# A hybrid decoder step on one core: sample gates loaded early by SyncE, middle tokens' norms ahead of the sample group's, output tiles stored in halves

## The chip, the core and the metric

The kernel runs on one core of a Trainium2 chip. The core has five engines with queues of their own: TensorE (PE in the profile; PEld is its weight load), VectorE (DVE), ScalarE (ACT), GpSimd (POOL) and SyncE (SP), and 16 DMA engines that they share. The metric is the device time of one execution in microseconds, from the chip's own clock; the kernel is timed over several runs, and one execution more is recorded by the hardware profiler.

## What is computed

One layer of a decoder with two kinds of attention heads side by side, for a prompt of 1024 new tokens and a sample group of 8 x 8 new tokens that have 4096 past tokens each. All data are float32. Cut to what matters here:

```python
def project(x, norm_g, w_in, q_g, ks_g, kw_g):
    h = rms_norm(x, norm_g)                 # over D_MODEL = 1024
    z = h @ w_in                            # 3864 columns
    (q_a, k_a, v_a, gate_a, q_b, kc, vc, ks, vs, kw, vw, br, gate_b) = jnp.split(z, split_at, axis=-1)
    ...
    br = jax.nn.sigmoid(br.reshape(B, T, NSA_HEADS, 3))

def decoder_layer(...):
    o_sb = stick_breaking(q_a, ...)         # over past and new rows
    o_nsa = nsa_attend(q_b, br, ...)        # gates br weigh compressed, selected and window attention
    u = concat([o_sb * silu(gate_a), o_nsa * silu(gate_b)])
    h = x + u @ w_out
    y = h + sigmoid(h @ w_ple_gate) * (p @ w_ple)
```

## The kernel before

The 1768.8 us fall into five stretches. Up to some 550 us `phase1` normalizes the tokens and multiplies them with `w_in`, from some 390 us on mixed with stick-breaking units of the prompt (`phase_d`). From 550 to 590 the prompt's rows are compressed (`prompt` in `phase_c`). From 590 to 985 `phase_c` goes through the eight sample sequences (batches of some 47 us): it gathers 1 MB pieces of the paged cache, compresses them and scores them. From 985 to 1510 come the stick-breaking attention of the sample group (`phase_b`) and the prompt's second kind of heads (the rest of `phase_d`), mixed. From 1510 on the output projections run (`a` and `b` of the last class).

**phase1.** The 1024 prompt tokens are nine tiles `x` with the sample group: tile 0 to 7 of 128 tokens, tile 8 of 64. `xnorm(ts)` (L135 on) normalizes one or two tiles: a square sum of the even one on ScalarE (L143), of the odd one on VectorE (L141), the small statistics on VectorE and ScalarE (L67 to L72), and the scaling on VectorE (L149) and GpSimd (L147). `xtrans(t0, n)` (L151 on) transposes two tiles on TensorE in eight k steps (L155); each step is then split into a high part `hh` (ScalarE, L157) and a low part `hl` (VectorE, L158). The matmuls of L278 multiply these with the weights, which `wsplit` splits into `whi` (GpSimd, L122) and `wlo` (VectorE, L123). In the text the order is: pair 0/1, pair 2/3, sample tile 8 with its transposes (L178) and split (L180 to L182), pair 4/5, pair 6/7.

**Gates of the sample group.** `phase1` writes the raw gates `br` to the scratch tensor `s_br_s`. At its start after the prompt's compression, `phase_c` makes two small tiles: `cgtc` (64 x 24) is filled by eight loads of 64 runs of 12 bytes each (L617, issued by ScalarE), `sigmoid_small` takes Exp on ScalarE (L57), add and reciprocal on VectorE (L58, L59), and four copies make `cgts` (L620). They are read in every batch. Around them stand ScalarE's table load for Tanh (L516), the casts XH (L491), GpSimd's or VectorE's XL (L496) and the matmuls H (L510).

**Output.** In `b` (L1709) two halves n of 512 columns are computed one after the other into one tile `y` (one buffer), and ScalarE issues one store of 512 KB a tile (L1726), 256 KB for the sample tile.

**What sets the order.** A scheduler that simulates the engines orders each engine's instructions, in the order in which they can start by its model. In `phase_c` from its start to the middle of batch 6 the order is written out by hand instead. SyncE and ScalarE issue the plain DMAs, GpSimd the gathers; the DMAs of SyncE and ScalarE share eight semaphores in turn, and a DMA waits until the earlier one on its semaphore has landed.

Of the kernel before, what the change touches and what calls it, by code (L numbers as in the profile page):

```python
# [5 lines left out]
F32 = mybir.dt.float32  # L6
# [14 lines left out]
def hbm(ap, off, dims):  # L21
    return bass.AP(tensor=ap.tensor, offset=ap.offset + off, ap=[list(d) for d in dims])
# [61 lines left out]
def phase1(K, beside=None):  # L84

    nc, A = K.nc, K.A
    with ExitStack() as es:
# [63 lines left out]
        def xtrans(t0, n):  # L151
            for k in range(8):
                pt = ps.tile([128, 512], F32, name="pt", bufs=2)[:, 0:n * 128]
                for i in range(n):
                    nc.tensor.transpose(pt[:, i * 128:(i + 1) * 128], xt[t0 + i][:, k * 128:(k + 1) * 128], K.id)  # L155
                o = slice(t0 * 128, (t0 + n) * 128)
                K.last_hh = nc.scalar.activation(hh[:, k, o], pt, AF.Copy, scale=gT[:, k:k + 1])  # L157
                nc.vector.scalar_tensor_tensor(hl[:, k, o], pt, gT[:, k:k + 1], hh[:, k, o].bitcast(F32), op0=OP.mult, op1=OP.subtract)  # L158
# [12 lines left out]
        for k in range(2, 8, 2):  # L171
            wsplit(0, k)
        xnorm([2, 3])
        xtrans(2, 2)
        xnorm([8])
        pt = ps.tile([128, 512], F32, name="pt", bufs=2)
        for k in range(8):
# [2 lines left out]
        nc.vector.tensor_tensor(tmp, pt.rearrange("p (k t) -> p k t", k=8), gT.unsqueeze(2).to_broadcast([128, 8, 64]), op=OP.mult)  # L180
        nc.scalar.copy(hs[:, :, 0:64], tmp)
        nc.vector.tensor_tensor(hs[:, :, 64:128], tmp, hs[:, :, 0:64].bitcast(F32), op=OP.subtract)  # L182
        for t in (4, 6):
            xnorm([t, t + 1])
            xtrans(t, 2)
        nc.vector.tensor_scalar(gq, gq, 0.125, None, op0=OP.mult)
        xes.close()

# [108 lines left out]
def c_consts(K, cst):  # L297


    nc, A = K.nc, K.A  # L300
# [4 lines left out]
    C.Qb = [cst.tile([128, 2, 2, 4, 4, 8], F32, name=f"cQb{i}") for i in range(2)]  # L305
    for t in C.Qb:
        V.memset(t, 0.0)
    C.W2 = cst.tile([128, 2, 2, 64], F32, name="cw2")
    for kv, n in enumerate("kv"):
        nc.scalar.dma_start(C.W2[:, kv], hbm(A["cmp_w2_" + n], 0, [[64, 128], [128 * 64, 2], [1, 64]]))  # L310
# [139 lines left out]
def phase_c(K, es, esr, tail, more):  # L450
# [160 lines left out]
    for t in kz + [VN]:  # L611
        G.memset(t, 0.0)

    gts = wk.tile([128, 8, 3], F32, name="cgts")
    gtc = wk.tile([64, 8, 3], F32, name="cgtc")
    for h in range(8):
        nc.scalar.dma_start(gtc[h * 8:h * 8 + 8], hbm(T["br_s"], h * 3, [[24, 8], [192, 8], [1, 3]]))  # L617
    sigmoid_small(K, gtc.rearrange("p a b -> p (a b)"))
    for p in range(4):
        V.tensor_copy(gts[p * 32:p * 32 + 32], gtc[(p // 2) * 32:(p // 2) * 32 + 32])  # L620
# [960 lines left out]
class Phase3:  # L1581
# [127 lines left out]
    def b(s, t):  # L1709
        K, A = s.K, s.K.A  # L1710
# [10 lines left out]
        for n in range(2):  # L1721
# [1 line left out]
            S_.activation(y[:m, c], s.product(HX, s.WG, n, 8, S)[:m], AF.Tanh, scale=0.5)  # L1723
            V.scalar_tensor_tensor(y[:m, c], y[:m, c], 1.0, s.product(PX, s.WP, n, 2, S)[:m], op0=OP.add, op1=OP.mult)
            V.scalar_tensor_tensor(y[:m, c], y[:m, c], 0.5, h[:m, c], op0=OP.mult, op1=OP.add)
        nc.scalar.dma_start(hbm(A["y_sample" if S else "y_prompt"], t * 131072 * (not S), [[1024, m], [1, 1024]]), y[:m])  # L1726


EV = tuple(int(x) for x in "1,1".split(","))
# [199 lines left out]
```

## Time and profile before

| | |
|---|---|
| median of 3 runs | 1770.9 us (1770.6 to 1770.93) |
| profiled execution | 1770.6 us |
| its span, first to last instruction | 1768.8 us |
| TensorE busy | 1593.8 us (90%) |
| VectorE busy | 1194.0 us (68%) |
| ScalarE busy | 882.9 us (50%) |
| GpSimd busy | 637.9 us (36%) |
| mean granted TensorE clock | 0.957 of full |

A row of a timeline gives start, duration, engine, line, operation, output and input, and in brackets the idle time before it with what ended it. `x4` joins four instructions of a kind; the duration then runs from the first start to the last end. Matmuls overlap, so their durations are longer than their distance from start to start. "PEclk" is the clock that was granted in a stretch, as a share of 2.4 GHz; 0.50 is 1.2 GHz. ACTq and SPq rows are DMA issues of ScalarE and SyncE.

### The profile page before, as it was taken

To read this page: it belongs to the slowest core of one execution; us is meant where nothing else is said; L and a number is where in the kernel's file an instruction comes from. 1 tells how busy PE (TensorE), PEld (TensorE's weight loads), DVE (VectorE), ACT (ScalarE), POOL (GpSimd) and SP (SyncE) were. 2 spreads that over 40 slices of the span, in tenths; PEclk is the share of its full clock that TensorE was granted. 3 is DMA by queue.
4 is the path that set the end of the run, shared out by engine and by line. 5 is a ranking of instruction groups with operands and counts; after the bars stand their busy time and mean duration, and the time that the engine had idled before them with its cause. 6 is when DMAs were issued, how large, how long until landed. Compare 5 with 4: busy or idle time off the path is not lost.

```text
span 1768.8 us, 41348 instructions
## 1 busy us (share of the span) xinstructions
PE 1593.8 (90%) x15742; PEld 1366.9 (77%) x15742; DVE 1194.0 (68%) x2540; ACT 882.9 (50%) x2220; POOL 637.9 (36%) x1059
## 2 busy tenths in 40 slices
PE   5999999999987799999999688998789887789998
PEld 5999898988876699899988456667567666668887
DVE  7336756877877578788888787676777865573322
ACT  4213645756667334444444478677678777221111
POOL 3123011132313455555553155355345455530000
PEclk9999999999988899999999699899999999799999
DMA  6235132131225465555554997787888874542210
GB/s 199 80 117 161 61 107 92 47 114 59 80 62 119 138 210 189 200 185 199 193 191 136 335 307 275 261 287 269 286 310 295 291 242 138 183 149 77 72 51 36
DMA packets 187080, 300.78 MB, mean 170 GB/s; under 512 B 30265, under 2 KB 100730, under 8 KB 178554
## 3 DMA queue, kind: packets, MB, share of 16 engines
q1 hardware_dynamic: 144930, 206.65, 35.6%
q0 software_dynamic: 9216, 67.11, 11.2%
q10 hardware_dynamic: 32736, 24.38, 4.3%
q8 instruction: 124, 2.03, 0.5%
q14 instruction: 74, 0.61, 0.1%
HBM read 271.81 MB, written 30.48 MB: 171 GB/s over the span
## 4 chain that ended last, share of the span: by engine, by line
PE 37%; DVE 14%; DMA 11%; ACT 6%; issue 5%; POOL 3%; SPq 1%; ACTq 0%; DVEq 0%; POOLq 0%
PE acc L1635 11%; PE H L510 5%; DMA bkv<-in_cache_sb 5%; DMA raw<-in_cache_nsa,cidx 3%; PE pt L1272 2%; PE bz L1394 2%; PE bo L1410 2%; DVE bkT L1488 2%; PE pt L1249 2%; PE sc L682 2%; ACT bAT L1539 1%; PE cav L824 1%; PE acc L278 1%; PE acc L276 1%; DVE xt L486 1%
## 5 line engine op out<-in xcount | busy, mean ns | idle before, releaser
L278 PE MATMUL acc<-whi,hh 128*128 128x256 f32 (+1 forms) x704 | 203.5, 290 | 4.1 <-DVE og L1768 2.5
L278 PE MATMUL acc<-wlo,hh 128*128 128x256 f32 (+1 forms) x704 | 201.0, 287 | 0.0
L278 PE MATMUL acc<-whi,hl 128*128 128x256 f32 (+1 forms) x704 | 199.6, 289 | 0.0
L1488 DVE STREAM_TRANSPOSE bkT<-bkv 128x1024 f32<-128x1024 f32 x128 | 157.5, 1236 | 53.8 <-DMA bkv<-in_cache_sb 37.2
L1240 POOL TENSOR_SCALAR t<-t,nst,gates 128x640 f32<-128x640 f32 (+7 forms) x128 | 107.4, 841 | 107.1 <-DVE nst L1236 71.2
L278 PEld LDWEIGHTS acc<-whi,hh 128*128 128x128 f32 x704 | 134.8, 192 | 6.8 <-POOL whi L122 2.9
L491 ACT CAST XH<-xt 128x512 fp32r<-128x512 f32 x128 | 79.1, 619 | 120.3 <-PE H L510 110.6
L278 PEld LDWEIGHTS acc<-wlo,hh 128*128 128x128 f32 x704 | 134.8, 192 | 0.2 <-issue 0.2
L278 PEld LDWEIGHTS acc<-whi,hl 128*128 128x128 f32 x704 | 132.4, 191 | 0.4 <-issue 0.3
L122 POOL TENSOR_SCALAR whi<-wraw 128x512 fp32r<-128x512 f32 (+1 forms) x60 | 54.0, 925 | 190.3 <-PE acc L248 154.6
L1249 PE MATMUL pt<-idf,t 128*128 128x128 f32 x528 | 95.1, 294 | 17.6 <-ACT u L1766 5.4
L1410 PE MATMUL bo<-bkv,bAT 128*16 128x128 f32 x2048 | 87.7, 289 | 22.5 <-POOL bAT L1541 16.9
L661 POOL DMA_INDIRECT raw<-in_cache_nsa,cidx x64 | 66.0, 1031 | 99.9 <-DVE xt L486 53.3
L1541 POOL TENSOR_SCALAR bAT<-baT 32x128 f32<-32x128 f32 x256 | 76.4, 298 | 71.1 <-DVE baT L1531 37.8
L1766 ACT COPY aT<-pt 128x512 f32<-128x512 f32 (+3 forms) x167 | 77.2, 475 | 35.6 <-PE pt L1050 19.8
L510 PE MATMUL H<-w1hk,XH 128*128 128x256 f32 (+1 forms) x272 | 86.1, 316 | 9.0 <-ACT XH L491 8.2
L1249 PEld LDWEIGHTS pt<-idf,t 128*128 128x128 f32 x528 | 60.5, 146 | 43.7 <-issue 14.2
L1410 PEld LDWEIGHTS bo<-bkv,bAT 128*16 128x16 f32 x2048 | 60.4, 101 | 41.5 <-POOL bAT L1541 27.2
L486 DVE STREAM_TRANSPOSE xt<-raw 128x512 f32<-128x512 f32 x132 | 88.1, 680 | 4.7 <-DMA raw<-out_nsa_rows_prompt 2.9
L1394 PE MATMUL bz<-bkT,bQ 128*32 128x128 f32 x2048 | 84.1, 290 | 7.9 <-DVE bkT L1488 4.5
L1094 DVE TENSOR_TENSOR_SCAN t<-ones,t 128x1024 f32<-128x1024 f32 (+7 forms) x64 | 88.2, 1380 | 0.7
L496 POOL TENSOR_TENSOR XL<-xt,XH 128x512 fp32r<-128x512 f32 x56 | 72.2, 1289 | 38.1 <-ACT XH L491 36.5
(467 smaller groups left out, 5003.1 us busy)
## 6 DMA issues: line engine op xcount, KB each, us to landing
bkv<-in_cache_sb SPq DMA_DIRECT2D x256, 512.0 KB
wraw<-in_w_in SPq DMA_DIRECT2D x28, 512.0 KB
x<-in_x_prompt SPq DMA_DIRECT2D x8, 512.0 KB
out_sb_rows_prompt<-o ACTq DMA_DIRECT2D x32, 128.0 KB
s_gT<-og ACTq DMA_DIRECT2D x16, 256.0 KB
cwin<-in_state_win SPq DMA_DIRECT2D x8, 512.0 KB
wr<-in_w_out SPq DMA_DIRECT2D x16, 256.0 KB
u<-s_uT SPq DMA_DIRECT2D x8, 512.0 KB
```

What stands on the lines that cost most here:

```text
L278: nc.tensor.matmul(acc[:, :w], a[:, k, t * 128:(t + 1) * 128], b[:, k, :w], start=i == 0, stop=i == 23)
L486: V.transpose(xt[:, :, e, :, b], raw[:, :, 0:256].rearrange("p l (k e c) -> p e l k c", e=2, c=32)[:, e])
L491: S_.copy(XH.rearrange("p a b -> p (a b)"), x.rearrange("p e k b s -> p (e k b s)"))
L510: nc.tensor.matmul(H[:m, kv * 256:kv * 256 + 256], x[:, c], y[:, l * 2 + e], start=start and l + kv + e + i == 0, stop=stop and l == 7 and ...
L1094: nc.vector.tensor_tensor_scan(a[:, ::-1], K.ones.to_broadcast([128, W]), a[:, ::-1], 0.0, op0=OP.mult, op1=OP.add)
L1240: (nc.vector if e == "V" else nc.gpsimd).tensor_scalar(x, x, st[:, j:j + 1], gate, op0=OP.mult, op1=OP.mult)
L1249: nc.tensor.transpose(pt[:, b * 128:(b + 1) * 128], x, K.id)
L1394: nc.tensor.matmul(z(h, g), q(j), kT(j), start=jj == 0, stop=jj == 1, skip_group_check=True, tile_position=(0, h * 32))
L1410: nc.tensor.matmul(oav[i * 32:i * 32 + 16], lhs(g, hp), v[:, i * 128:i * 128 + 128], start=first, stop=last, skip_group_check=True, tile_p ...
L1488: V.transpose(t.kT[f][:, :, i % 4:i % 4 + 2].rearrange("p j i t -> p i j t"), kv[:, k:k + 2].rearrange("p i (j c) -> p i j c", j=16))
L1635: nc.tensor.matmul(acc, a, b, start=i == 0, stop=i == len(terms) - 1)
L1766: S_.copy(o, i)
```

## The change

Three edits. In `phase1` the norms of pair 4/5 and 6/7 stand ahead of the sample tile's, the transposes of pair 4/5 directly behind those of pair 2/3, and those of pair 6/7 behind the sample tile's. In `phase_c` the two gate tiles come from the pool of constants and not from the stage's working pool, and the eight loads are issued by SyncE. In `b` the store of a tile becomes two stores of 512 columns, each behind its half, the first by SyncE and the second by ScalarE.

```diff
@@ phase1
         xnorm([2, 3])
+        xnorm([4, 5])
         xtrans(2, 2)
+        xnorm([6, 7])
+        xtrans(4, 2)
         xnorm([8])
...
-        for t in (4, 6):
-            xnorm([t, t + 1])
-            xtrans(t, 2)
+        xtrans(6, 2)
@@ c_consts
+    C.gts = cst.tile([128, 8, 3], F32, name="cgts")
+    C.gtc = cst.tile([64, 8, 3], F32, name="cgtc")
@@ phase_c
-    gts = wk.tile([128, 8, 3], F32, name="cgts")
-    gtc = wk.tile([64, 8, 3], F32, name="cgtc")
+    gts, gtc = C.gts, C.gtc
     for h in range(8):
-        nc.scalar.dma_start(gtc[h * 8:h * 8 + 8], hbm(T["br_s"], h * 3, [[24, 8], [192, 8], [1, 3]]))
+        nc.sync.dma_start(gtc[h * 8:h * 8 + 8], hbm(T["br_s"], h * 3, [[24, 8], [192, 8], [1, 3]]))
@@ b
-        nc.scalar.dma_start(hbm(A["y_sample" if S else "y_prompt"], t * 131072 * (not S), [[1024, m], [1, 1024]]), y[:m])
+            (nc.sync, nc.scalar)[n].dma_start(hbm(A["y_sample" if S else "y_prompt"], t * 131072 * (not S) + n * 512, [[1024, m], [1, 512]]), y[:m, c])
```

The scheduler makes of it an order that differs on all engines at the edited places, and beyond them in two stretches, from some 400 to 590 us and from 985 to 1510 us. The matmuls of `phase_c`'s hand-written part stand as before. Line numbers of the changed kernel are one to three higher.

VectorE in `phase1`, around the second pair's k steps. Before, the splits of the second pair (L158) and of the sample tile (L180, L182) come first, then the norms of the middle pairs (L141 to L149):

```order
L158 SCALAR_TENSOR_TENSOR hl<-pt,gT,hh 128x256 x6
L180 TENSOR_TENSOR junk<-pt,gT 128x512
L141 ISA junk,xss<-x 128x1024
L141 ISA xss 128x1
L182 TENSOR_TENSOR hs<-junk,hs 128x8x64
L67 TENSOR_SCALAR rs<-xss 128x2
L141 ISA junk,xss<-x 128x1024
```

and now the square sums stand between the first pairs' `hl`:

```order
L158 SCALAR_TENSOR_TENSOR hl<-pt,gT,hh 128x256
L67 TENSOR_SCALAR rs<-xss 128x2
L158 SCALAR_TENSOR_TENSOR hl<-pt,gT,hh 128x256
L141 ISA junk,xss<-x 128x1024
L141 ISA xss 128x1
L158 SCALAR_TENSOR_TENSOR hl<-pt,gT,hh 128x256
L70 TENSOR_TENSOR rs<-rs 128x2
```

Two square sums, three groups of statistics and four scalings now lie among the ten `hl` ahead of the third pair's, instead of behind all of the second pair's.

SyncE at 384 us (`nat` are query and key rows of a stick-breaking pair, `vn` its value rows, `wraw` weights of phase1). Before:

```order
L980 DMA nat<-s_qa_p 128x4x128 x2
L980 DMA nat<-out_sb_rows_prompt 128x4x128 x2
L115 DMA wraw<-in_w_in 128x4x256 x4
L1056 DMA vn<-out_sb_rows_prompt 128x8x128
L1111 DMA s_uT<-u 128x1024
```

and now:

```order
L982 DMA nat<-s_qa_p 128x4x128 x2
L982 DMA nat<-out_sb_rows_prompt 128x4x128 x2
L115 DMA wraw<-in_w_in 128x4x256 x2
L619 DMA cgtc<-s_br_s 8x8x3 x8
L115 DMA wraw<-in_w_in 128x4x256 x2
L1058 DMA vn<-out_sb_rows_prompt 128x8x128
```

The eight gate loads stand ahead of the last two weight loads. On ScalarE they stood at 590 us, ahead of the table load:

```order
L1096 ACTIVATE t_5628<-t_5628 128x512
L1766 COPY aT<-pt 128x512
L617 DMA cgtc<-s_br_s 8x8x3 x8
L516 ACT_TABLE_LOAD
L516 ACTIVATE chs<-H 64x512
L491 CAST XH<-xt 128x512 x2
L57 ACTIVATE cgtc<-cgtc 64x24
```

and ScalarE's order there is now:

```order
L1098 ACTIVATE t_5630<-t_5630 128x512
L1768 COPY aT<-pt 128x512
L519 ACT_TABLE_LOAD
L519 ACTIVATE chs<-H 64x512
L494 CAST XH<-xt 128x512 x2
L528 COPY chT<-pt 128x4x64
```

Loads and Exp are gone from it; the Exp of L57 now stands some 310 rows earlier, at about 394 us of the time before.

GpSimd at the end of the mixed stretch (`t` and `cz` are weights of prompt heads, `bAT` the stick-breaking weights of the sample group, `woh` the output weights). Before:

```order
L1522 TENSOR_TENSOR ba<-ba,bos 128x512
L1240 TENSOR_SCALAR t_21512<-t_21512,nst,gates 128x640
L1240 TENSOR_SCALAR cz_12668<-cz_12668,nst,gates 128x32
L1240 TENSOR_SCALAR t_21523<-t_21523,nst,gates 128x640
L1541 TENSOR_SCALAR bAT<-baT 32x16x8 x8
L1240 TENSOR_SCALAR t_21554<-t_21554,nst,gates 128x640
L1240 TENSOR_SCALAR cz_12668<-cz_12668,nst,gates 128x32
L1240 TENSOR_SCALAR t_21586<-t_21586,nst,gates 128x640
L1622 TENSOR_SCALAR woh_21422<-wr 128x512 x5
```

and now:

```order
L1524 TENSOR_TENSOR ba<-ba,bos 128x512
L1543 TENSOR_SCALAR bAT<-baT 32x16x8 x8
L1242 TENSOR_SCALAR t_21512<-t_21512,nst,gates 128x640
L1242 TENSOR_SCALAR cz_12668<-cz_12668,nst,gates 128x32
L1242 TENSOR_SCALAR t_21523<-t_21523,nst,gates 128x640
L1624 TENSOR_SCALAR woh_21422<-wr 128x512 x5
L1242 TENSOR_SCALAR t_21554<-t_21554,nst,gates 128x640
```

The last `bAT` and the five `woh` each stand ahead of three rows that they stood behind.

## Rows read from the trace of the kernel before

**Rows 1.** The page, part 2: TensorE's busy tenths in 40 slices.

```profile
PE   5999999999987799999999688998789887789998
```

**Rows 2.** Stretches of phase1: span, length, busy time (instructions) by engine, PEclk, DMA share, GB/s.

```profile
16.00:34.00 18.00, 17.12 (x129) 16.26 (x129) 12.49 (x31) 9.70 (x24) 4.10 (x5) 1.00 0.63 188
...
36.00:38.00 2.00, 0.00 (x0) 0.00 (x0) 1.93 (x7) 1.17 (x6) 0.44 (x1) 0.65 0.29 98
...
42.00:44.00 2.00, 2.00 (x13) 2.00 (x13) 0.48 (x1) 0.81 (x2) 0.00 (x0) 0.64 0.00 0
```

**Rows 3.** Timeline of TensorE from 34 us.

```profile
34.00 0.39 PE L278 MATMUL acc<-whi,hl 128*128 128x256 f32 x2
38.39 0.66 PE L155 MATMUL pt<-idf,x 128*128 128x128 f32 x2 [4.00 <-DVE rs L70]
...
43.34 0.52 PE L278 MATMUL acc<-whi,hl 128*128 128x256 f32 x2
...
44.16 0.38 PE L155 MATMUL pt<-idf,x 128*128 128x128 f32 x2
...
44.73 0.28 PE L278 MATMUL acc<-wlo,hh 128*128 128x256 f32 x1
...
45.08 0.38 PE L155 MATMUL pt<-idf,x 128*128 128x128 f32 x2
```

**Rows 4.** Timeline of VectorE, second pair's splits and a middle pair's norm.

```profile
30.61 0.48 DVE L158 SCALAR_TENSOR_TENSOR hl<-pt,gT,hh 128x256 fp32r<-128x256 f32 x1 [0.44 <-ACT hh L157]
...
35.76 1.23 DVE L141 CUSTOM_DVE_ANT_0 junk<-x 128x1024 f32<-128x1024 f32 x1
...
36.91 0.16 DVE L70 TENSOR_TENSOR rs<-rs 128x2 f32<-128x2 f32 x1
...
37.49 0.75 DVE L149 TENSOR_SCALAR x<-x,rs 128x1024 f32<-128x1024 f32 x1
```

**Rows 5.** Timeline of ScalarE from 590 us.

```profile
590.80 11.01 ACTq L617 DMA_DIRECT2D cgtc<-s_br_s  x8
601.89 1.28 ACT L516 ACT_TABLE_LOAD   x1 [10.53 <-DMA cgtc<-s_br_s]
```

**Rows 6.** The chain that ended last, 585 to 612 us: start, share of it, what.

```profile
601.54 2.24 DMA cgtc<-s_br_s
```

**Rows 7.** Timeline of all engines, 594 to 608 us.

```profile
594.38 0.67 DVE L486 STREAM_TRANSPOSE xt<-raw 128x512 f32<-128x512 f32 x1
...
602.25 0.71 DVE L669 STREAM_TRANSPOSE xk<-raw 128x512 f32<-128x512 f32 x1 [7.20 <-DMA raw<-in_cache_nsa,cidx]
...
604.34 0.58 PE L510 MATMUL H<-w1hk,XH 128*128 128x256 f32 x1 [8.22 <-ACT XH L491]
...
606.71 1.35 DVE L620 COPY cgts<-cgtc 32x24 f32<-32x24 f32 x4
...
608.00 1.05 PE L682 MATMUL sc<-xk,cQb 128*128 128x128 f32 x4
```

**Rows 8.** Stretches of 2 us in phase_c, columns as in group 2.

```profile
598.00:600.00 2.00, 0.00 (x0) 0.00 (x0) 0.00 (x0) 0.00 (x0) 0.00 (x0) 0.95 0.93 363
...
608.00:610.00 2.00, 2.00 (x11) 1.79 (x10) 1.34 (x3) 0.62 (x1) 1.27 (x2) 0.50 0.39 78
```

**Rows 9.** Timelines of SyncE and of ScalarE, 384 to 391 us.

```profile
384.12 39.31 SPq L115 DMA_DIRECT2D wraw<-in_w_in  x4
...
390.84 0.33 ACTq L284 DMA_DIRECT2D s_gT<-og  x1
```

**Rows 10.** Timeline of VectorE at 570 us, the prompt's rows.

```profile
570.30 1.30 DVE L486 STREAM_TRANSPOSE xt<-raw 128x512 f32<-128x512 f32 x2 [2.89 <-DMA raw<-out_nsa_rows_prompt]
```

**Rows 11.** Timeline of ScalarE at the end.

```profile
1765.18 0.34 ACTq L1726 DMA_DIRECT2D out_y_prompt<-y  x1
```

**Rows 12.** A stretch of the tail, columns as in group 2.

```profile
1766.50:1767.00 0.50, 0.00 (x0) 0.00 (x0) 0.00 (x0) 0.00 (x0) 0.00 (x0) 1.00 1.06 434
```

**Rows 13.** TensorE's waits, 985 to 1500 us: sum, times, longest.

```profile
PE bo L1410 <- POOL bAT L1541: 16.9, 17, 2.5
```

## The prediction

> **What bounds the kernel now.** I read the profile from the outside in: first the page's forty slices, then TensorE's idle time with what released it, then every engine around the places that the diff touches. TensorE sets the time. Its slices are nearly full from start to end [rows 1], with dips where other engines hold it up; a microsecond counts only if it comes out of such a dip, or out of the tail after TensorE's last matmul. The profiled execution took 1770.6 us, of which 1768.8 is the span and 1.8 lies around it; it is 0.3 below the median of the three runs, so the sum below is made against 1770.6 and 0.3 is added at the end.
>
> Three dips belong to the change. The first is at 34 us: the last matmul of the second token pair begins at 34.00 and ends at 34.39, and the next thing TensorE does is the transpose at 38.39, held 4.00 us by the norm of tokens 4 and 5 [rows 3]. The clock is granted 0.65 in 36 to 38, that is between its two levels, and 0.64 in 42 to 44, after standing at 1.2 GHz [rows 2]. The second is at 596 us: ScalarE's table load waits 10.53 us for the gate request `cgtc` [rows 5], its cast XH comes behind that, and TensorE waits 8.22 us for XH [rows 7]; the clock is granted 0.95 in 598 to 600 and still stands at 1.2 GHz (0.50) in 608 to 610 [rows 8]. The third is the tail: the last store is issued at 1765.18 [rows 11] and the span ends at 1768.8.
>
> **The change part by part.**
>
> *Middle tokens' norms (dip 1).* From 34.39 to 43.34 [rows 3] TensorE does only ten matmuls and eight transposes. At full clock three matmuls take 0.35 (44.73 to 45.08), a k step of two transposes and six matmuls 0.92 (44.16 to 45.08) [rows 3], so a matmul is 0.117 and a transpose 0.11; ten and eight make 2.05. If both norms are done in time, 8.95 - 2.05 = 6.9 us go away, waits and half clock together. That is the upper end.
>
> The work doesn't vanish: it moves into 16 to 34. On VectorE a norm of two tokens is 1.23 (square sum), 0.75 (scaling) and five small operations of 0.08 to 0.17, 0.72 together [rows 4]: 2.7 each, 5.4 for two. VectorE is busy 12.49 of those 18 us [rows 2], so 5.5 are free, just what is wanted, but in pieces of 0.44 between the `hl` subtractions that wait for ScalarE's `hh` [rows 4], while a square sum of 1.23 fits no such piece. The small operations fit the pieces; each square sum overruns its piece by 1.23 - 0.44 = 0.79 and each scaling by 0.75 - 0.44 = 0.31, and TensorE's k step waits for the `hl` behind: 2 x 0.79 + 2 x 0.31 = 2.2 us late. So I take 6.9 - 2.2 = **4.7**. The lower bound is 1.5: all 5.4 us turn into TensorE waits. ScalarE's two square passes and GpSimd's two scalings also move; both engines are more than 40% idle there [rows 2]. The sample group's square pass, transposes and subtraction move behind the middle pair's; they issue no DMA, and cost nothing as long as TensorE has matmuls to do beside them. After 43 us TensorE has no dip to swallow the gain until some 390 us [rows 1].
>
> *Sample gates (dip 2).* The eight small loads go to SyncE, asked for at 384 instead of 590, and ScalarE has nothing before its table load and XH. The last `xt` that XH needs is written at 594.38 + 0.67 [rows 7]; the load of the table (1.28, [rows 5]) then lies in ScalarE's idle time. By estimate from these rows, XH is ready at 596.2, GpSimd's XL at 598.1, and the first twelve matmuls are through at about 599.3. What is late next are the two gathers that land at 602.25 [rows 7], which ScalarE never held: GpSimd issued them at 593.5 and 595.8. So the score matmuls of 608.00 can start at 602.25 + 0.71 = 602.96, 5.0 earlier [rows 7]. TensorE will have been idle some 3.7 us before that, about as long as the 4.00 of dip 1. If the clock falls as it did there, TensorE runs at 1.2 GHz for the 5.6 us from the first matmul at 604.34 to 610 [rows 7, 8], of which only 2.0 lay behind the start at 608.00: half of 3.6 is lost, and 3.2 stay. GpSimd's second XL, which the next gather stands behind, waits for the same landing and moves about as far. If the clock stays up, 5.0 + 1.0 = 6.0. I take **4.0**, near the lower end, because of the idle time's length.
> By the Trainium skill, "DMA: Bandwidth & Descriptors", section "Issuing engines are not separate DMA queues", a DMA issued from another engine runs on the same 16 DMA engines, and spreading the issuing saves only the sequencer's issue time. By that the move would be worth eight issues of 0.33 ([rows 9] has one), 2.6, and the sum would end 1.4 higher. This trace speaks for more: ScalarE stood 10.53 us [rows 5], far beyond issuing, and the gain comes from asking 200 us earlier. Nothing else here hangs on that page.
>
> *What the gates cost at 384 to 405.* SyncE issues four weight loads from 384.12 on, the last pair long waiting for a buffer [rows 9]; the eight requests now stand ahead of that pair. Behind them in SyncE's queue are only this pair and later loads; eight issues of a third of a microsecond fit into the wait. Each needs a DMA slot freed, the latest by the store issued at 390.84 [rows 9]. ScalarE's Exp now stands at about 394, and VectorE's six small operations (four copies of 1.35 together [rows 7], two smaller ones, under 2 us) at about 397, in front of a head norm that feeds a store of window keys. If the gates have landed, it costs 0 to 2, and the last needs 2.24 to land as its fellow did [rows 6], till about 393.1, just ahead of the Exp. I take **+0.5**, with 0 and 2 + 2.24 as ends. The same operations go away at 606, beside TensorE's matmuls.
>
> *Prompt rows.* SyncE's loads near 550 change places: three more row loads stand ahead of the first four `w_cmp_v` loads, and two behind it go earlier. A wait of 2.89 for rows [rows 10] may shrink by what weights get later: 0, with 1.5 to either side.
>
> *Output halves.* Half of each tile leaves some 4 us sooner; in the tail only the second half, 256 KB, is left to move after 1765.18 [rows 11]. At the 434 GB/s of that stretch [rows 12] half a tile is **0.6** less; the wait before the data moves and after it stays. Nine more issues stand on SyncE, which waits for a VectorE result in the middle of loads due tens of microseconds later; no cost. From 0.3 to 0.7.
>
> *Order.* The order of all engines also changes where nothing was edited, in 400 to 590 and in 985 to 1510, because the scheduler breaks ties anew. On GpSimd the stick-breaking weights `bAT` or a neighbour stand elsewhere at some ten places of the later stretch. TensorE waited there for `bAT` 17 times for 16.9 in all, 1.0 a time, 2.5 at most [rows 13]. The sign is open: 0, with four places at 1.0 to either side.
>
> Sum: -4.7 - 4.0 + 0.5 - 0.6 = -8.8; 1770.6 - 8.8 = 1761.8, and 0.3 more against the median: **1762.1**.
>
> **The rivals.**
> *The clock stays up.* In dip 2 the two idle pieces are parted by the twelve matmuls. For it: before, the clock was granted 0.95 over the first part of the 8.22 us wait [rows 8]. Against: in dip 1 it was already falling in the fourth microsecond of idling [rows 2, 3]. The gates give 6.0 instead of 4.0, and with a late `hl` chain costing only 1 us in dip 1 the norms 5.9: 1758.9, and down to 1756 if the new order helps by 3.
> "TensorE: Matmul & The Clock Gate", section "What's actually happening", of the Trainium skill, has activity release the throttle, which would let those matmuls count; no row of this trace shows such a case.
> *Norms only change their place.* The 5.4 us on VectorE stall TensorE one for one in 16 to 34. For it: no free piece there is long enough. Against: 5.5 us are free in sum. Gain 1.5 instead of 4.7: 1765.3.
> *The new order of the late stretch costs.* GpSimd works in queue order, and a `bAT` behind a `t` that waits for VectorE holds the output matmuls. If five of the ten places lose the longest wait, 2.5 [rows 13], that is 12.5: 1762.1 + 12.5 = 1774.6, slower than before. It turns slower than before from four places on. For it: these are the commonest waits there. Against: a new tie is as likely to take such a wait away, and most moves are by one unit. If only the gain is eaten, the time is within 1767 to 1774.
>
> **How the numbers follow.** 0.2% of this kernel, 3.5 us, is what a measurement can tell from no change. Forecast (1758.5 to 1765): 0.53. Clock stays up: 0.15. Norms only change place: 0.14. Order eats the gain, within 0.2%: 0.11; slower by more: 0.07. So faster 0.82, same 0.11, slower 0.07. The range leaves out about one in ten at each side: 1755 holds both upper ends with some help from the order, 1769 the lower bounds of both dips with some loss.
>
> **What would show it.** Norms right: no wait of over 1 us for a norm at 34, the clock at 1.00 through 30 to 45, and a few `hl` waits of half a microsecond in 20 to 32. Wrong: the same idle time spread there. Gates right: no ScalarE wait for `cgtc`, XH near 596, the next wait of TensorE or VectorE for `raw` near 593 to 594 of the new time. Wrong: the score matmuls come less than 3 us sooner, or Exp waits for `cgtc` near 390. Halves right: 0.3 to 0.7 us less from VectorE's last result to the end. Order: the stretch from 985 to the first output projection matmul (L1635) takes up to 4 us more or less. The forecast is wrong as a whole if that last number is larger than both dips' gain.

## The result, and the profile after

The changed kernel took 1750.3 us (median of 4 runs, 1745.2 to 1755.5) against 1770.9 for the kernel before on the same chip: a ratio of 0.989, with 0.986 to 0.992 as its interval. The forecast was 1762.1, with a range of 1755 to 1769. The direction was right, but the gain, 20.6 us, is more than twice the 8.8 that the sum gave. The profiled execution of the changed kernel took 1745.2, its span is 1743.4, so between the two profiles there are 25.4 us to account for. Runs of one kernel spread by some 10 us (1745.2 to 1755.5 here), so a piece read from one profile of each is uncertain by microseconds; where sizes matter below, medians of runs on one chip or means over several profiles decide.

The page of the changed kernel, parts 1 and 2, answers to [rows 1]:

```profile
PE 1583.6 (91%) x15742; PEld 1364.4 (78%) x15742; DVE 1190.5 (68%) x2540; ACT 880.4 (50%) x2220; POOL 633.0 (36%) x1059
...
PE   5999999999997899999999689898898878789998
...
PEclk9999999999997999999999689999899999899999
```

TensorE is still the bound, with as many matmuls as before in 10 us less of busy time (1593.8 before), since fewer run at the lower clock: the mean is 0.963 against 0.957.

To see where the 25.4 us are, I divided both traces at the same instructions: the group of `whi` (L122) of phase1 near 412 us, the third gather of `phase_c`, the first key transpose `bkT` out of `bkv` (VectorE) of the mixed stretch, the first `uh` (GpSimd) of the output projections, and VectorE's fourth finished output row `y`. The table gives the length of each piece, so a row's sum is the span; its last column is the median of the runs.

| kernel | to `whi` at 412 | to 3rd gather | to `bkT` | to `uh` | to 4th `y` | to the end | span | median |
|---|---|---|---|---|---|---|---|---|
| before | 412.7 | 180.8 | 385.7 | 529.3 | 97.8 | 162.5 | 1768.8 | 1770.9 |
| changed | 411.6 | 176.7 | 379.0 | 524.4 | 89.6 | 162.1 | 1743.4 | 1750.3 |
| difference | -1.1 | -4.1 | -6.6 | -4.9 | -8.2 | -0.4 | -25.4 | |
| forecast | -4.2 | 0 ± 1.5 | -4.0 | 0 ± 4 for two | | -0.6 | -8.8 | |

The forecast's -4.2 is the norms' -4.7 and the gates' +0.5. Half of the gain, 13.1, stands in the two pieces from `bkT` to the fourth `y` (979 to 1606 us before), where nothing was edited and the forecast had zero.

**The norms, up to 57 us.** TensorE's timeline of the changed kernel and stretches of it, in the columns of [rows 2, 3]:

```profile
27.49 0.44 PE L155 MATMUL pt<-idf,x 128*128 128x128 f32 x2 [1.76 <-DVE hl L158]
...
28.64 0.48 PE L155 MATMUL pt<-idf,x 128*128 128x128 f32 x2 [0.48 <-DVE hl L158]
```

```profile
16.00:34.00 18.00, 14.81 (x95) 13.61 (x94) 16.21 (x41) 9.29 (x27) 8.33 (x7) 0.91 0.54 147
...
26.00:28.00 2.00, 0.51 (x4) 0.47 (x4) 2.00 (x6) 0.04 (x1) 1.52 (x2) 1.00 0.00 0
28.00:30.00 2.00, 1.52 (x10) 1.36 (x9) 2.00 (x9) 1.46 (x4) 0.64 (x1) 0.73 0.43 69
30.00:32.00 2.00, 2.00 (x11) 2.00 (x11) 2.00 (x3) 0.27 (x1) 0.48 (x1) 0.50 0.96 307
```

The wait of 4.00 us for a norm at 38 is gone. In its place VectorE is full from 24 to 32, a square sum makes the `hl` behind it 1.76 us late, and after the lightly loaded 26 to 28 the clock is granted 0.73 and then 0.50, the lower of its two levels. The third pair's `whi`, a fixed point behind dip 1, starts at 57.33 instead of 59.58.

**The gates.** ScalarE, GpSimd and TensorE of the changed kernel around 590, which answers to [rows 5, 7], and SyncE's and ScalarE's rows at 387 and 393:

```profile
386.91 4.71 SPq L619 DMA_DIRECT2D cgtc<-s_br_s  x8
```

```profile
393.12 0.22 ACT L57 ACTIVATE cgtc<-cgtc 64x24 f32<-64x24 f32 x1
```

```profile
586.95 1.28 ACT L519 ACT_TABLE_LOAD   x1 [1.69 <-PE pt L1108]
...
588.27 1.00 POOL L663 DMA_INDIRECT raw<-in_cache_nsa,cidx  x1 [0.27 <-POOL cvs L673]
...
590.61 1.14 ACT L494 CAST XH<-xt 128x512 fp32r<-128x512 f32 x2 [1.77 <-DVE cimp L631]
```

```profile
597.11 0.71 PE L684 MATMUL sc<-xk,cQb 128*128 128x128 f32 x4 [1.73 <-DVE xk L671]
```

There is no wait for `cgtc`. Seen from the third gather (593.50 before, 588.27 now), XH starts 2.3 us later instead of 10.2, and the score matmuls 8.8 instead of 14.5. ScalarE's Exp at 393 waits for nothing.

**The loads of the prompt's rows.** Two pieces of the chain of waits, of before and then of the changed kernel (start, share, what):

```profile
547.92 2.10 DMA s_g_s<-o
...
558.50 6.48 DMA wraw<-in_cmp_w_v
565.00 4.88 DMA raw<-out_nsa_rows_prompt
```

```profile
534.27 2.05 DMA s_g_s<-o
...
547.11 5.98 DMA raw<-out_nsa_rows_prompt
```

SyncE's first row load starts as the store of phase1's last gates (`s_g_s`) has landed, at 550.21 before and at 536.41 now: in the new order of 457 to 540 that store comes 13.7 us earlier. The `w_cmp_v` weights are off the chain, and the prompt's compression is through 4 us sooner.

**The handover to the output projections.** Before, TensorE's timeline and two stretches:

```profile
1516.16 1.97 PE L1272 MATMUL pt<-aT,vs 128*64 128x128 f32 x16 [4.72 <-ACT aW L1766]
1526.02 0.69 PE L1654 MATMUL pt<-idf,u 64*128 64x64 f32 x4 [5.13 <-DVE us L1657]
```

```profile
1510.00:1520.00 10.00, 4.89 (x44) 4.34 (x42) 9.48 (x10) 2.73 (x5) 9.38 (x8) 0.73 0.83 258
...
1520.00:1530.00 10.00, 4.87 (x20) 3.68 (x17) 5.88 (x8) 1.86 (x4) 5.53 (x4) 0.50 0.44 133
```

and the changed kernel's:

```profile
1496.64 1.09 PE L1251 MATMUL pt<-idf,t 128*128 128x128 f32 x4 [4.12 <-ACT u L1768]
1500.63 0.69 PE L1656 MATMUL pt<-idf,u 64*128 64x64 f32 x4 [2.90 <-DVE u L1699]
1503.04 1.98 PE L1274 MATMUL pt<-aT,vs 128*64 128x128 f32 x16 [0.46 <-ACT aW L1768]
```

```profile
1494.00:1504.00 10.00, 3.99 (x23) 3.10 (x25) 9.48 (x10) 4.14 (x8) 9.08 (x7) 0.63 0.61 198
...
1504.00:1514.00 10.00, 10.00 (x63) 8.51 (x60) 5.20 (x8) 1.64 (x4) 2.62 (x4) 0.86 0.40 118
```

Here the mixed stretch has run out of matmuls and the projections have not begun. Before, TensorE is half idle from 1510 to 1530 with the clock going down to its lower level; now the half-idle stretch is over at 1504, in an order in which the sample group's transposes (`idf,u`) run ahead of the last value matmuls (`aT,vs`) instead of behind them. It is near the place where GpSimd's last `bAT` and the five `woh` went ahead in the order. The whole piece from `uh` to the fourth `y`, before and then now:

```profile
1508.48:1606.28 97.80, 81.99 (x378) 65.46 (x375) 60.79 (x76) 17.07 (x31) 34.37 (x33) 0.88 0.46 145
```

```profile
1491.70:1581.35 89.65, 76.80 (x370) 61.32 (x365) 60.58 (x76) 17.37 (x31) 32.51 (x34) 0.94 0.49 155
```

Of the 8.2 us, 3.0 are less idle time of TensorE (15.8 before, 12.8 now) and 5.2 less busy time, at a higher mean clock (0.94 against 0.88).

**The tail.** The last store answers to [rows 11]:

```profile
1740.44 0.34 ACTq L1728 DMA_DIRECT2D out_y_prompt<-y  x1
```

From the end of VectorE's last result to the end of the span it is 2.98 us (1740.41 to 1743.39), 3.65 before.

### The profile page after: what moved, and what is told of

The parts are those of the page before. It is cut to its first block, busy times and chain, and to the rows that moved or that the text cites. A ratio compares the mean times of both kernels' runs of the same rounds, so it can differ in the third digit from the quotient of the medians.

```text
span 1743.4 us, 41364 instructions
## 1 busy us (share of the span) xinstructions
PE 1583.6 (91%) x15742; PEld 1364.4 (78%) x15742; DVE 1190.5 (68%) x2540; ACT 880.4 (50%) x2220; POOL 633.0 (36%) x1059
## 4 chain that ended last, share of the span: by engine, by line
PE 40%; DVE 13%; DMA 12%; ACT 6%; issue 4%; POOL 2%; SPq 1%; ACTq 0%; DVEq 0%; POOLq 0%
PE acc L1637 11%; PE H L513 6%; DMA bkv<-in_cache_sb 5%; DMA raw<-in_cache_nsa,cidx 4%; PE acc L279 2%; PE pt L1274 2%; PE bz L1396 2%; PE bo L1412 2%; PE pt L1251 2%; DVE bkT L1490 2%; PE sc L684 1%; PE cav L826 1%; ACT bAT L1541 1%; PE acc L277 1%; DVE bs L1512 1%
## 5 line engine op out<-in xcount | busy, mean ns | idle before, releaser
L1242 POOL TENSOR_SCALAR t<-t,nst,gates 128x640 f32<-128x640 f32 (+7 forms) x128 | 106.7, 835 | 94.7 <-DVE nst L1238 51.9
L122 POOL TENSOR_SCALAR whi<-wraw 128x512 fp32r<-128x512 f32 (+1 forms) x60 | 54.0, 925 | 198.2 <-PE acc L249 183.8
L1412 PE MATMUL bo<-bkv,bAT 128*16 128x128 f32 x2048 | 84.2, 287 | 14.3 <-POOL bAT L1543 10.0
L1204 DVE CUSTOM_DVE_ANT_0 t<-z,bx 128x1024 f32<-128x1024 f32 (+7 forms) x96 | 73.9, 770 | 16.9 <-PE z L1040 16.4
```

The costliest lines, as they stand in the source:

```text
L1242: (nc.vector if e == "V" else nc.gpsimd).tensor_scalar(x, x, st[:, j:j + 1], gate, op0=OP.mult, op1=OP.mult)
L1412: nc.tensor.matmul(oav[i * 32:i * 32 + 16], lhs(g, hp), v[:, i * 128:i * 128 + 128], start=first, stop=last, skip_group_check=True, tile_p ...
```

## The experiments

Two theories stood at the start. By the **edit theory** the three edits give the 20 us, each more than forecast. By the **order theory** they give about what was forecast, and the rest comes from the scheduler's other order in the long stretches that nobody edited. Each kernel was profiled and timed on one chip with the kernel before; ratios are to that kernel.

**Each edit alone.**

```diff
 e1_halves_only, in b of the kernel before
-        nc.scalar.dma_start(hbm(A["y_sample" ...], t * 131072 * (not S), [[1024, m], [1, 1024]]), y[:m])
+            (nc.sync, nc.scalar)[n].dma_start(hbm(..., t * 131072 * (not S) + n * 512, [[1024, m], [1, 512]]), y[:m, c])
 e2_norms_only, in phase1 of the kernel before
+        xnorm([4, 5])
         xtrans(2, 2)
+        xnorm([6, 7])
+        xtrans(4, 2)
...
 e3_gates_only, the kernel before with the two tiles from the constants and
-        nc.scalar.dma_start(gtc[h * 8:h * 8 + 8], ...)
+        nc.sync.dma_start(gtc[h * 8:h * 8 + 8], ...)
 e4_gates_const_by_scalar, the kernel before with the tiles alone: ScalarE still issues the loads
-    gts = wk.tile([128, 8, 3], F32, name="cgts")
-    gtc = wk.tile([64, 8, 3], F32, name="cgtc")
+    gts, gtc = C.gts, C.gtc
```

> Only the output tiles' stores are halved; every engine's order up to the output stage is that of the kernel before. Order theory (a large part of the gain comes from the mixed stretch 985 to 1510, whose order any edit shakes up) and edit theory (each edit earns its own part wherever it stands, the stretch only follows): both say 0.5 to 0.7 us less than before, all of it behind VectorE's last result, and the mixed stretch within 1 us of before. If halves gained more than 2 us, both are wrong.

> Only the norms of the middle pairs move; the wait for the gate loads at 590 stays. The order of the mixed stretch is a third one, neither that of before nor that of after. Both theories: 2.2 us less by 60 us, as in the changed kernel, and the 10 us wait of ScalarE at 590 still there. Edit theory: 1768 to 1769 in all, the mixed stretch within 2 us of before's length. Order theory: the mixed stretch's length moves by several us either way, so the total is anywhere from 1758 to 1775.

> Only the gates: kept among the constants and asked for by SyncE at 384. The order of the mixed stretch is a fourth one. Both theories: 5 to 6 us gained between 588 and 610, some 1 us lost at 390. Edit theory: 1765 to 1767, mixed stretch within 2 us of before. Order theory: mixed stretch different by several us, total 1755 to 1772.

> The gates kept among the constants, but asked for by ScalarE as before (its loads now stand near 388 us); norms and stores as before. The order of the mixed stretch is, on GpSimd, exactly that of the changed kernel. Order theory: the mixed stretch is shorter than before by what it is in the changed kernel, 8 to 13 us, and with 4 to 6 from the gates the total is 1752 to 1759. Edit theory: 1765 to 1767, mixed stretch as before. That ScalarE's asking early is as good as SyncE's would show in ScalarE's wait at 590 being gone.

Measured: the halves 1.001 (0.999 to 1.003), the norms 1.009 (1.007 to 1.012), the gates by SyncE 0.999 (0.997 to 1.001), the gates among the constants but asked for by ScalarE 0.991 (0.988 to 0.994). Alone, two edits change nothing that can be told, one makes the kernel slower, and a part of the gates' edit takes 16.3 us off, more than two thirds of what the whole change does. Parts that add up to +0.9% cannot make -1.1% by themselves. Pieces as above (us, median in the last column):

| kernel | to `whi` at 412 | to 3rd gather | to `bkT` | to `uh` | to 4th `y` | to the end | median |
|---|---|---|---|---|---|---|---|
| e1 halves | 413.5 | 185.1 | 387.2 | 535.6 | 94.3 | 162.8 | 1774.1 |
| e2 norms | 411.6 | 186.4 | 387.7 | 550.0 | 96.4 | 162.5 | 1789.4 |
| e3 gates | 414.4 | 180.0 | 381.8 | 539.8 | 94.7 | 162.6 | 1771.3 |
| e4 gates, ScalarE | 414.5 | 177.2 | 384.4 | 530.1 | 93.5 | 162.5 | 1756.6 |

Each edit does its part where it stands: the norms shorten the first column, the gates the third. What decides the total lies mostly in the fourth, which runs from 530 to 550 and which no edit touches. The kernel before took 1772.9 in these runs. Three expectations missed. e1's mixed stretch took 535.6 in an order that had not changed, where both theories had before's length within 1 us. e2's 1789.4 lies above all that the order theory allowed (1775). e4's mixed stretch is not shorter than before, though its order is nearly the changed kernel's; its handover is shorter (93.5), but its profiled run, 1764.1, is 7.5 above its median, so the pieces do not show where its 16.3 us come from.

**The edits without the late order, and the changed kernel again.**

```diff
 e5_all_edits_old_order, from the changed kernel
-        nc.sync.dma_start(gtc[h * 8:h * 8 + 8], ...)
+        nc.scalar.dma_start(gtc[h * 8:h * 8 + 8], ...)
```

With ScalarE issuing the gate loads, near 388, the scheduler gives VectorE and GpSimd from 985 on the order that they had before the change. `e6_changed_kernel_again` is the changed kernel unaltered.

> All three edits, but the early gate loads are issued by ScalarE instead of SyncE. In the mixed stretch the order of every engine is that of the kernel before (VectorE and GpSimd without a difference). Order theory: the front and the tail gain what they gain in the changed kernel, 8 to 11 us, and the mixed stretch is as long as before: 1760 to 1763 on a chip where before takes 1771. Edit theory (the gain of the changed kernel belongs to its edits): as fast as the changed kernel on the same chip, within 2 us.

> The changed kernel itself, on the chip of the other three. Both theories: 18 to 24 us less than before, run to run spread of several us.

Measured: e5 0.994 (0.992 to 0.996), 1762.5; e6 0.988 (0.985 to 0.992), 1750.7; the kernel before 1774.4. So all three edits in the late order of before are worth 11.9, and the changed kernel 23.7. Not all of the other 11.8 belongs to the late order: who issues the gate loads differs too, and with it the order from 400 to 590. Of the 13.8 between the two profiled executions 3.7 lie ahead of `bkT` (0.5 at 412 us, 1.8 up to the third gather, 1.5 up to `bkT`) and 10.1 behind it: 2.3 up to `uh`, 7.0 in the handover, 0.8 in the tail. TensorE's waits of e5 from 1470 to 1535, and then e6's (sum, times, longest):

```profile
PE pt L1656 <- DVE us L1659: 5.1, 1, 5.1
PE pt L1274 <- ACT aW L1768: 4.8, 1, 4.8
```

```profile
PE pt L1251 <- ACT u L1768: 3.5, 1, 3.5
PE pt L1656 <- DVE u L1699: 3.4, 1, 3.4
```

e5 repeats both long waits of before, e6 those of the changed kernel. From `uh` to the fourth `y` e5 takes 98.6 and e6 91.6. The direction holds in every profile: with the late order of before that piece takes 97.8, 94.3 (e1) and 98.6; with that of the changed kernel, or nearly so, 89.6, 91.6 (e6), 90.9 (e7), 91.7 (e8) and 93.5 (e4). By the means the two orders are 5.4 apart there. The piece before it, `bkT` to `uh`, takes 529.3, 535.6 and 524.3 with the one order and 522.0 to 530.1 with the other; one order alone spreads by 11, so these profiles can't tell whether the order changes anything there.

**Who asks for the gates, and when; and the norms' share.**

```diff
 e7_gates_late_by_sync, from the changed kernel
...
-    gts, gtc = C.gts, C.gtc
+    gts = wk.tile([128, 8, 3], F32, name="cgts")
+    gtc = wk.tile([64, 8, 3], F32, name="cgtc")
 e8_const_gates_and_halves, from the changed kernel
-        xnorm([4, 5])
         xtrans(2, 2)
-        xnorm([6, 7])
-        xtrans(4, 2)
...
-        nc.sync.dma_start(gtc[h * 8:h * 8 + 8], ...)
+        nc.scalar.dma_start(gtc[h * 8:h * 8 + 8], ...)
```

In e7 the late order is the changed kernel's; SyncE issues the gate loads at 594, in the stage that reads them. In e8 it is nearly the changed kernel's, the norms stand as before, and ScalarE issues the gate loads, early.

> The changed kernel with the gate tiles back in the stage's working pool: SyncE issues the eight loads, but only near 590; Exp stands behind the casts XH and the first score sums. In the mixed stretch every engine's order is that of the changed kernel. If what counts is that ScalarE is not held (my reading), the dip at 596 is gone here too, but SyncE's loads of the batch (cwin, ckz) stand behind the gates: 0 to 3 us slower than the changed kernel. If what counts is asking 200 us earlier: 4 to 6 us slower. If issuing from another engine saved the issue time alone: 2.6 us better than ScalarE's late issuing, so some 3 us slower than the changed kernel, with XH still late.

> The gates among the constants and asked for by ScalarE, the halves, but the norms as before; in the mixed stretch the changed kernel's order on GpSimd, and nearly so on the others. Order theory: the changed kernel's time plus what its norms earn, 2 to 3 us. Edit theory: plus 2 to 3 us as well, if the mixed stretch's gain hangs on the gates; plus 10 or more if it hangs on the norms or on SyncE's issuing.

Measured: e7 0.992 (0.989 to 0.994), 1759.3, 8.6 above e6; e8 0.990 (0.987 to 0.994), 1755.8, 5.0 above e6, which with these intervals is not clear of the noise. ScalarE's and SyncE's timelines of e7:

```profile
593.96 2.92 SPq L618 DMA_DIRECT2D cgtc<-s_br_s  x8
```

```profile
596.39 1.14 ACT L492 CAST XH<-xt 128x512 fp32r<-128x512 f32 x2 [1.72 <-DVE cimp L630]
```

From the third gather to the tenth, the local measure of dip 2, it is 38.7 in the kernel before, 33.6 in the changed one, and 33.3 in e7. So ScalarE's not standing in the queue gives the 5 us at dip 2, and asking 200 us ahead adds nothing there. The wait has not only moved to another engine. In e7 SyncE issues the eight loads one behind the other, ahead of its own `ckz` loads for the batch, in 2.92 us; before, ScalarE issued them in 11.01 us [rows 5] while SyncE issued its loads of the batch between them, and the last one of ScalarE, at 601.54, had waited for one of these (`ckz`) to land. Over all profiles the measure is 33.6 to 36.4 in the eight that ask early and 38.7 to 39.6 in the four in which ScalarE asks late; the means are 4.3 apart. What e7 lacks against the changed kernel, more than any of its expectations had, is mostly elsewhere: from `whi` at 412 to the third gather it takes 183.9, like every kernel that asks for the gates in `phase_c` (180.8 before, 185.1, 186.4, 183.3), while those that ask early take 175.0 to 177.2, and once 180.0 (e3). Its chain of waits shows why:

```profile
546.99 3.21 DMA raw<-out_nsa_rows_prompt
...
552.54 6.67 DMA wraw<-in_cmp_w_v
559.23 4.73 DMA raw<-out_nsa_rows_prompt
```

The `w_cmp_v` weights are on the chain, as before. The early gate loads are followed by an order in which the prompt's row loads start by 540 instead of after 543; in 13 profiles there is no exception. That the early row loads shorten the piece is the likely reading and not more: e3 has them at 539 and takes 180.0, with the `w_cmp_v` weights on its chain all the same. Why the scheduler ties the two was not found.

**A tile that nobody reads.**

```diff
 e9_changed_plus_32_bytes: the changed kernel, and among the constants
+    K.pz = cst.tile([128, 8], F32, name="pz")
+    V.memset(K.pz, 0.0)
 e10_before_plus_384_bytes: the kernel before, and among the constants
+    K.pz = cst.tile([128, 96], F32, name="pz")
+    V.memset(K.pz, 0.0)
```

Neither computes anything else; 32 and 384 bytes a partition move later tiles, and the late order changes.

> The changed kernel with one tile of 8 floats more a partition among the constants and one memset of it: no work to speak of. Up to the sample stage all orders are the changed kernel's; in the mixed stretch and the handover to the output stage the order is yet another. Order theory: the front as in the changed kernel, then several us to either side of its 536 to 540 (first key transpose to last) and of its handover: total 1745 to 1768, not within the spread of the changed kernel by rule. Edit theory: the changed kernel's time, 1750 where before takes 1774.

> The kernel before with one tile of 96 floats more a partition among the constants and one memset: none of the three edits. Orders as before up to the sample stage, another one in the mixed stretch and the handover. Order theory: several us off before's time, either way (1760 to 1785 where before takes 1774), all of it after 960 us. Edit theory: before's time within 0.2%.

Measured: e9 1.003 (1.001 to 1.005), 1778.6, 1.5% or some 26 us above the changed kernel; e10 1.007 (1.004 to 1.009), 1783.9 against 1773.3 for the kernel before. Up to `bkT` e9 is as early as the changed kernel (968.7 against 967.3), then it takes 553.7 to `uh` instead of 524.4; e10 takes 547.0. TensorE's and GpSimd's timelines of e9 at 1020, and a stretch:

```profile
1020.76 0.61 PE L1414 MATMUL bo<-bkv,bAT 128*16 128x128 f32 x2 [13.19 <-POOL bAT L1545]
```

```profile
1018.36 3.80 POOL L1545 TENSOR_SCALAR bAT<-baT 32x128 f32<-32x128 f32 x8 [10.86 <-DVE gates L1139]
```

```profile
1010.00:1020.00 10.00, 0.00 (x0) 0.00 (x0) 7.36 (x13) 4.49 (x12) 1.52 (x3) 0.50 1.12 271
1020.00:1030.00 10.00, 8.98 (x150) 6.97 (x154) 4.47 (x6) 5.17 (x18) 5.44 (x16) 0.64 0.79 236
```

One wait of 13.19 us, with the clock at 0.50 and then 0.64 behind it, five times the longest wait for a `bAT` before (2.5, [rows 13]). It is not the third rival's mechanism, though it ends in the same wait: no `t` stands ahead of this `bAT`, and GpSimd had been idle for 10.86 us. Ahead of `bAT` comes VectorE's transpose `baT` (1017.54), ahead of that ScalarE's `ba` (1015.85), and ScalarE stood still for 9.21 us while it issued loads of prompt rows, two of which waited until one of SyncE's `bkv` loads had landed (at 1008.16 and 1012.78):

```profile
1005.35 7.82 ACTq L1024 DMA_DIRECT2D nat<-out_nsa_rows_prompt  x3
...
1014.30 0.21 ACT L883 COPY co<-sB 64x64 f32<-64x64 f32 x1 [9.21 <-DMA nat<-out_nsa_rows_prompt]
```

That is what dip 2 was, at another place. e10 has the same: ScalarE stands for 10.54 us until 1028.08 at the same loads, and TensorE waits 13.69 until 1034.82. In the other eleven profiles ScalarE issues these loads by 971, in some 2.5 us. In the waits of the mixed stretch e10's wait stands out, and the changed kernel has none like it (e10, then the changed kernel):

```profile
PE bo L1412 <- POOL bAT L1543: 27.1, 14, 13.7
```

```profile
PE bo L1412 <- POOL bAT L1543: 10.0, 14, 1.4
```

So the edit theory falls: the late stretch moves by as much as the whole gain, here both times for the worse, with nothing changed but where tiles lie and the order that follows. e9's total lies above the order theory's 1745 to 1768, e10's inside its range. The one wait is not all of e9's 29 us in the mixed stretch; the rest was not traced.

**The second norm behind all `hh` of the second pair.**

```diff
 e11_second_norm_later, from the changed kernel
-        xnorm([6, 7])
+        with K.tc.issue_after(K.last_hh.ins):
+            xnorm([6, 7])
```

> The changed kernel, but the norm of the second middle pair is held back until the second pair's last high part is written, so that it falls among the third pair's k steps. The mixed stretch has again another order, so the front is read at 57 us, where the changed kernel stands 2.2 us ahead of before. If the waits for `hl` and the fall of the clock at 28 us ate the other half of the gain, no wait of over 0.6 us and a clock of 1.00 between 26 and 34, and 4.5 to 6 us ahead at 57 us. If VectorE's work itself was the limit: 2 to 3 us ahead as now. Total 1745 to 1768, by the order.

Measured: 0.993 (0.990 to 0.996), 1762.2. It does what it is for, in part: the third pair's `whi` starts at 55.96 instead of 57.33, 3.6 ahead of before and so between the two expectations, TensorE's clock is 1.00 through 24 to 34, and a wait of 1.1 is left. But the late order is another again, with 535.0 from `bkT` to `uh`, and the 1.4 us are lost many times over. TensorE's waits from 12 to 57 us, of e11, e6, the changed kernel and the kernel before:

```profile
PE pt L155 <- DVE hl L158: 2.1, 2, 1.1
```

```profile
PE pt L155 <- DVE hl L158: 4.5, 5, 1.8
```

```profile
PE pt L155 <- DVE hl L158: 3.1, 4, 1.8
```

```profile
PE pt L155 <- DVE hl L158: 0.9, 2, 0.4
```

No version beat the changed kernel.

## Why the prediction was wrong, step by step

**Order, "0, with four places at 1.0 to either side": the step that failed.** It measured -13.1 between the two profiles, and -9.3 (2.3 and 7.0) between e5 and e6, whose edits differ only in who issues the gate loads. Two things were wrong with it. It took its unit from one kind of wait, TensorE for `bAT` [rows 13]; those shrank from 16.9 to 10.0, which alone is more than the 4 that the term allowed, though how much of it reached the length of the mixed stretch can't be told. Above all the order was also different at the handover, which the front part shows on GpSimd and the prediction's sum never priced: waits of 4.72 and 5.13 with half clock around them stood there, and 8.2 us went away, 5.4 by the means of the two orders. And it took the longest wait of before as the most that a place can cost; e9 and e10 have one of 13. With the handover's two waits in view the bound would, by estimate, have been some 10 us to the good side, and the range would have held 1750. The prediction's own sign, the stretch up to the first output projection matmul, came out 7.4 shorter (547.5 from `bkT` before, 540.1 now) where it allowed 4. In the rival that loses by the order, it was right that another order can cost more than the gain, as e9 shows, but by ScalarE's loads and not by a `t` in GpSimd's queue. Here the lot fell the other way.

**Prompt rows, "0, with 1.5 to either side": mis-sized.** The wait for rows went from 2.89 to 2.2 us, as was allowed; but the whole stretch that ends in it was 4.1 shorter, in an order in which the row loads start 13.7 us sooner. The prediction looked at the wait and not at what released the first load (`s_g_s`).

**Gates, 4.0: right in size, more in the one profile.** Between the two profiles the piece from the third gather to `bkT` is 6.6 shorter; at dip 2 itself 5.1 by the tenth gather. By the means of the eight profiles that ask early and the four in which ScalarE asks late it is 4.4 and 4.3. In the profile of the changed kernel the clock helps. Columns as in [rows 8], before and then the changed kernel:

```profile
600.00:640.00 40.00, 34.12 (x254) 32.53 (x255) 23.91 (x46) 14.61 (x30) 22.42 (x29) 0.84 0.55 189
```

```profile
600.00:640.00 40.00, 36.18 (x293) 34.45 (x292) 24.18 (x47) 14.12 (x27) 25.38 (x33) 1.00 0.65 215
```

The idle time is in pieces of at most 1.73 us with matmuls between them, and the clock stays at 1.00, as the first rival has it. But that is one execution. In e6, the same kernel again, the longest wait there is 1.72 and the clock falls all the same:

```profile
596.00:600.00 4.00, 4.00 (x24) 3.99 (x23) 2.66 (x6) 1.10 (x2) 1.63 (x3) 0.57 0.41 99
```

From the third gather to `bkT` e6 takes 379.7, hardly more than the 379.0 of the other execution. So whether the clock stays up here differs from run to run, and the first rival's 6.0 is not shown. One reading behind the choice was off as well: 0.65 over 36 to 38 [rows 2] puts the fall of the clock in dip 1 at 36.6, in the third microsecond of idling and not the fourth. That activity releases the throttle, which the Trainium skill has in "TensorE: Matmul & The Clock Gate", section "What's actually happening", agrees with e6: TensorE is busy in all of 596 to 600, and from 600 to 610 the clock is at 1.00. The estimate of 2.6 by the Trainium skill's "DMA: Bandwidth & Descriptors", section "Issuing engines are not separate DMA queues", is too small here: e7, where at this place the issuing engine changed and with it the loads' place among SyncE's, gains 5.4. The prediction's reason for more than that, asking 200 us ahead, was wrong all the same: what counts is that ScalarE no longer stands waiting in its queue.

**What the gates cost at 384 to 405, 0.5: nothing.** The two traces stand 1.06 apart at 380, ahead of the loads, and 1.09 at 412.

**Norms, 4.7: mis-sized.** At 57 us the changed kernel is 2.25 ahead of the profile of before. Over twelve profiles the third pair's `whi` starts at 59.6 to 60.9 in the six with the old norms and at 56.6 to 57.7 in the six with the new ones, 3.1 apart by the means. The 6.9 that go away were right: no wait for a norm is left. The 2.2 for late `hl` were too few. In e6, where the clock stays up, `hl` waits go from 0.9 to 4.5, 3.6 more; in the changed kernel they go to 3.1 only, because TensorE at half clock doesn't catch up with VectorE. Both reach the same point, at 57.36 and 57.33, so the clock's fall cost nothing here: VectorE, 16.21 of 18 us busy, sets the pace. Between the two profiles 1.0 of the gain goes again ahead of 380, with a wait of 1.39 for `hraw` at 376.60 instead of 0.38 at 377.66; over the twelve it does not, and at 412 us the two sixes are still 3.1 apart. e8 puts the norms' worth in the whole kernel at 5.0, but it is not free of other order or of noise either. By the means the second rival, that the norms only change place (1.5), was as far too low as the 4.7 was too high.

**Halves, 0.6: right in the changed kernel, not in each.** There it is 0.67 less from VectorE's last result to the end; in e1, e5 and e8 it is 0.3 more (last section), and alone the halves gave nothing that can be told.

So the mechanisms of the edits were right in the main, and by pieces of the two profiles the edits themselves give -2.2, 0, -6.6 and -0.7, 9.5 against 8.8. By the means over all profiles the norms give 3.1 and the gates 4.4. That the sum comes out so well between these two profiles is luck: the norms were taken too high, and the gates look larger there than they are by the means. (The 11.9 of e5 have the earlier row loads in them as well.) The time was missed by the order of what nobody edited.

## What to carry to other kernels

Where a scheduler orders the work, an edit has two effects, its own and that of the new order elsewhere; measure them apart, with a version that keeps the edit and the old order and one that changes the order and nothing else, before giving an edit the credit or the blame. A term for "order" is priced from the longest idle places of the bound engine in the stretches that are reordered, the handover between two stages first of all, and its bad end is not the longest wait seen so far. Loads that an engine with compute behind them issues can hold that compute: ScalarE stood still for 10.53 us before the change, and for 9.21 and 10.54 in e9 and e10, while its loads waited for earlier ones to land. They are better placed where no compute stands behind them. A wait's last releaser is followed back from engine to engine before a cause is named; TensorE's wait for GpSimd in e9 began on ScalarE. Square sums put between small pieces of work cost more than their overruns here (3.6 us of `hl` waits instead of 2.2), with VectorE busy 16.2 of 18 us.

## What was not expected of the hardware

In three kernels the span ends later than the data would have it. e1, e5 and e8 store the output in halves as the changed kernel does, and the packets of their last store begin as early (0.9 us behind VectorE's last result), but the last of them ends at 2.1 us instead of 1.7, and the span 3.9 us behind that result instead of 3.0. The DMA queues of the last 3.9 us of e5, and of the last 3.0 of the changed kernel (packets, MB, share):

```profile
q10 hardware_dynamic: 144, 0.26, 18.2%
q14 instruction: 1, 0.01, 0.5%
```

```profile
q10 hardware_dynamic: 144, 0.26, 23.3%
```

One packet of the instruction queue, from 1.8 to 2.1 us behind VectorE's last result, lies in the tail of e1, e5 and e8 and not in that of the changed kernel. Whether it is the cause was not tried.

And the stretch from `bkT` to `uh` took 524 to 536 us in three profiles with one and the same order (before, e1, e5); what makes it differ from one execution to the next stays open, as does what is left of the 11.8 us between e5 and e6 beside the handover.
